# Two layers of a conv-FFN backbone on one core: raw operands kept and products chained in PSUM around the down-projection

## The chip, the cores and the metric

The kernel runs as one program on one NeuronCore of a Trainium2 chip. The metric is the device time of one execution in microseconds. The five engines work side by side, each in the order in which its own instructions were recorded: TensorE (PE), VectorE (DVE), ScalarE (ACT), GpSimd (POOL) and SyncE (SP, which here only issues DMAs). They wait for one another by semaphores. DMAs are issued from SP, from ACT and from POOL; those from POOL go to queue q0, which can add what it moves to what lies at the destination ("accumulate" below), the others to q1.

## The reference

Two layers. Each has a token-mixing sub-layer (attention, a gated linear recurrence, a Fourier mix) and then the gated ConvFFN that the change touches:

```python
def conv_ffn(h, w_up, conv_w, conv_b, w_down):
    u = h @ w_up                                   # 1024 -> 2 x 2816
    up = jnp.pad(u, ((0, 0), (1, 1), (0, 0)))
    u = up[:, :-2] * conv_w[0] + up[:, 1:-1] * conv_w[1] + up[:, 2:] * conv_w[2] + conv_b
    a, g = jnp.split(u, 2, axis=-1)
    return (a * jax.nn.silu(g)) @ w_down           # 2816 -> 1024

    x1 = layer_norm(ALPHA * x + g1 * mix, ln1_g[l], ln1_b[l])
    ffn = conv_ffn(x1 * (1 + sc2) + sh2, w_up[l], conv_w[l], conv_b[l], w_down[l])
    x = layer_norm(ALPHA * x1 + g2 * ffn, ln2_g[l], ln2_b[l])
```

There are 1024 latent tokens and 256 context tokens, all in float32. The change is in the ConvFFN of the latent tokens.

## The kernel before

**Arithmetic.** A float32 product is made of three passes of a reduced type. Every operand is split into a rounded part, hi (a cast on ACT), and the rest, lo (a subtraction), and `mm3` (L156 to L160) issues lo·hi, hi·lo and hi·hi. One such product of a 128x128 and a 128x512 tile is three matmuls.

**Two stages with seven products.** Both matrix products of the FFN are done as a 2x2 block product with seven block products in place of eight: A11..A22 are quarters of one operand, B11..B22 of the other, S1..S4 and T1..T4 are sums of quarters. The up-projection comes first, for 22 column pairs j, then the down-projection.

**Up-projection** (`up_weights`, `up_all`). For each j the weights are the A side. `operand` (L1204) makes S1 to S4 on DVE, `splits` casts hi on ACT (L1216) and subtracts lo on POOL (L1217). The B side, the tokens, lies in SBUF already split. Each product is 12 matmuls into one PSUM bank "p" of 128x512 (`up_product`). ORDER (L1186) has the products as A11, A12, S1, S2, S3, A22, S4. `up_all` then forms the outputs by seven DVE sums (L1232) of a bank and a part of the SBUF tiles U[0] and U[1] (each 128x1026: an early half of 512 tokens, a late half, and borders), after ACT has copied A11's bank to U[0]'s late half (L1265). `gate(j)` reads U: a width-3 convolution (`conv`: one ACT operation L1102, then two DVE operations L1105, for each of four half tiles), SiLU on ACT, and a DVE product (L1244 or L1246), whose result is stored to DRAM as `act`. For j below EARLY=6 the products A11 and A12 were made earlier (`up_early`), stored in DRAM ("parked") and are loaded to U[0]'s late half (L1259, L1271), one after the other. PE gets the operands up to five products ahead.

**Down-projection** (`down_operands`, `down_all`). The operands are now `act` (A side) and w_down (B side), each quarter 11 chunks of 128 rows, 2.88 MB. Seven phases run one after the other, in the order of DOWN (L1287): P1 = A11·B11, P7 = S3·T3, P6 = S2·T2, P4 = A22·T4, P5 = S1·T1, P3 = S4·B22, P2 = A12·B21. Each has six steps (one chunk, then five times two), of 12 matmuls for each chunk, into four PSUM banks; so a phase is 132 matmuls. A raw operand is loaded to a rotating buffer ("raw" for weights, "araw" for activations, three of these). Operands that are sums are held in SBUF: X (weights) and Y (activations), six tiles each. In P1 `hold` (L1322, L1326) loads X with B22 and Y with A11 and adds B12 and A21 by accumulate DMAs from POOL (L1319). Each later sum comes from the one before by one more accumulate DMA (`next_sum`), issued after the step's split has read the tile. S1 and T1, in P5, are a load into araw and into raw and an accumulate onto each. Splits are a cast on ACT (L1347) and a subtraction on DVE (L1348). At the end of a phase `combine` reads the four banks: a copy on ACT in P1 (L1403), sums on DVE (L1371) later. PLAN (L1428) has `load_r` load the residual rows r of the later four token tiles in steps 2 to 5 of P1 and multiply and add on DVE (L997, L998).

The order on each engine is the order of the recorded program, in which a recording layer hoists splits and sums ahead of the matmuls that use them; no engine passes an instruction that waits.

Of the kernel before, what the change touches and what calls it, by code (L numbers as in the profile page):

```python
# [11 lines left out]
F32 = mybir.dt.float32  # L12
# [84 lines left out]
def hybrid_backbone_kernel(ctx: ExitStack, tc: tile.TileContext, A: dict, out: bass.AP):  # L97
# [1072 lines left out]
    def up_product(w, b, bank):  # L1170
        acc = psu([P, HALF], "pu", bank)
        for k in range(4):
            mm3(acc, tuple(t[:, k, :] for t in w), tuple(t[:, k, :] for t in b), k == 0, k == 3)
# [12 lines left out]
    ORDER = (("A11", "B11"), ("A12", "B21"), ("S1", "T1"), ("S2", "T2"), ("S3", "T3"), ("A22", "T4"), ("S4", "B22"))  # L1186

    def up_weights(l, fp):
# [19 lines left out]
        def splits(todo):  # L1208
            for n, (j, nm) in enumerate(todo):
# [7 lines left out]
                nc.gpsimd.tensor_tensor(out=lo, in0=src, in1=f32(hi), op=ALU.subtract)  # L1217
# [5 lines left out]
    def up_all(l, fp, todo, ws, h, parked, act, bg):  # L1223
# [25 lines left out]
        for j, a, b in todo:  # L1249
            if a == [o for o in ORDER if j >= EARLY or o[0][0:2] != "A1"][0][0]:  # L1250
                p1, u2, u3, u4 = U[0][:, late], U[1][:, early], U[1][:, late], U[0][:, early]

                sums = (("u2", u2, "S2", "p1", ALU.add, ()), ("C11", p1, "A12", "p1", ALU.add, ("u2",)),
                        ("u3", u3, "S3", "u2", ALU.add, ()), ("u4", u4, "S1", "u2", ALU.add, ()),
                        ("C22", u2, "S1", "u3", ALU.add, ("u4",)), ("C21", u3, "u3", "A22", ALU.subtract, ("C22",)),
                        ("C12", u4, "S4", "u4", ALU.add, ()))
                got = {"p1": p1}
# [8 lines left out]
            for o, dst, x, y, op, after in sums:
                if o not in got and all(n in got for n in (x, y) + after):
                    add(dst, got[x], got[y], op)
                    got[o] = dst
                    if o == "u2" and j < EARLY:  # L1270
# [20 lines left out]
    def down_operands(l, f1, f2, f3, act):  # L1291
        X, Y = {}, {}
# [13 lines left out]
        def load_w(fw, q, ks):  # L1306
            count[0] += 1
            t = (fw if count[0] % 2 else wp).tile([P, 1024], F32, tag="raw", bufs=2, name="raw")[:, 0:512 * len(ks)]
            nc.sync.dma_start(out=halves(t), in_=w_part(q, ks))
            return t  # L1310

        def load_a(q, ks, eng=None, first=False):
            t = (wp if first else f1[0]).tile([P, 1024], F32, tag="raw" if first else "araw", bufs=2 if first else 3,
                                              name="araw")[:, 0:512 * len(ks)]
            (eng or nc.sync).dma_start(out=halves(t), in_=a_part(q, ks))
            return t
# [5 lines left out]
        def hold(n, ks):  # L1322

            for held, pl, nm, part, x, y in ((X, f3[0], "X", w_part, "B22", "B12"), (Y, f2[0], "Y", a_part, "A11", "A21")):
                held[n] = pl.tile([P, 512 * len(ks)], F32, tag=f"{nm}{n}", bufs=1, name=nm)
                nc.sync.dma_start(out=halves(held[n]), in_=part(x, ks))  # L1326
                plus(held[n], part(y, ks))

        def side_a(q, n, ks, first):
            if q[0] == "A":  # L1330
                return load_a(q, ks, nc.scalar if q == "A11" and n < 2 and not first else None, first)
            return plus(load_a("A22", ks), a_part("A21", ks)) if q == "S1" else Y[n]

        def side_b(fw, q, n, ks):
            if q[0] == "B":
                return load_w(fw, q, ks)
            return plus(load_w(fw, "B11", ks), w_part("B12", ks)) if q == "T1" else X[n]

        def next_sum(q, n, ks):
            if q in ("S3", "S2"):  # L1340
                plus(Y[n], a_part("A22" if q == "S3" else "A12", ks))
            if q in ("T3", "T2"):
                plus(X[n], w_part("B11" if q == "T3" else "B21", ks))
# [7 lines left out]
        def split_w(fw, q, n, ks):  # L1351
# [13 lines left out]
    def down_all(l, fp, fa, ops, ready, y1, rows, finish, deferred, halfway):  # L1365
# [65 lines left out]
        for x, (p, qa, qb) in enumerate(DOWN):  # L1431
# [385 lines left out]
```

## Time and profile before

| | |
|---|---|
| median of 3 runs | 3408.84 us (3407.7 to 3414.72) |
| profiled execution | 3419.26 us, span 3417.4 us |
| PE busy | 3116.8 us (91%) |
| DVE busy | 2417.0 us (71%) |
| ACT busy | 1550.2 us (45%) |
| POOL busy | 1261.6 us (37%) |
| POOL, lo of the up-projection (L1217) | 176 from S of 1618 ns mean, 108 from raw of 1392 ns |
| queue q1 | 409.24 MB |
| queue q0 (accumulates among it) | 55.80 MB |
| up-projection, layer 0 and layer 1 | about 895 to 1405 us, about 2680 to 3133 us |
| down-projection, layer 0 and layer 1 | about 1405 to 1680 us, about 3133 to 3417 us |

Read the engines' totals as averages over stages with different limits. The stage rows come from the trace: a stretch of time with the busy time of each engine in it, the groups by line, the waits (who waited for whom, how long, how often, the longest), the chain that ended last, and the timeline of one engine.

### The profile page before, as it was taken

The page shows a single profiled execution, that of the slowest core. Times are in us where ns is not written, and L with a number is a line of the kernel's source. Part 1 is how long each engine was busy: PE and PEld are TensorE (multiplying, and loading weights), DVE is VectorE, ACT ScalarE, POOL GpSimd, SP SyncE. Part 2 cuts the span into 40 slices and gives each one's busy share as a digit, 9 for nine tenths or more (in the row PEclk, how much of TensorE's full clock was granted, in tenths as well). Part 3 has the DMA queues.
Part 4 walks back from the last instruction along what each step waited for, and adds up shares of the span by engine and source line. Part 5 has one row for each costly group of instructions (what it writes and reads, how often), then busy time and mean ns, then how long its engine had stood idle before and what let it go on. Part 6 is the DMA issues. An engine that isn't in the chain of part 4 may idle for free.

```text
span 3417.4 us, 55716 instructions
## 1 busy us (share of the span) xinstructions
PE 3116.8 (91%) x20897; PEld 2540.3 (74%) x20897; DVE 2417.0 (71%) x4171; ACT 1550.2 (45%) x3105; POOL 1261.6 (37%) x1134
## 2 busy tenths in 40 slices
PE   6999998989889999798899999998978889998896
PEld 4879976778766777576798888876766668776675
DVE  4614568887698888547876755668877798886568
ACT  4325556664443433233465435655642434443332
POOL 3522105422464444241235341115435545553323
PEclk9999999999989999899999999998998899999898
DMA  7643122117764443698775432122035642225993
GB/s 214 204 153 85 49 93 58 40 44 220 224 183 142 129 129 122 192 246 205 242 209 178 131 105 70 47 90 65 21 112 159 195 130 74 79 81 159 255 227 123
DMA packets 457412, 468.60 MB, mean 137 GB/s; under 512 B 32244, under 2 KB 343989, under 8 KB 457143
## 3 DMA queue, kind: packets, MB, share of 16 engines
q1 hardware_dynamic: 422294, 409.24, 37.9%
q0 software_dynamic: 34848, 55.80, 8.6%
q8 instruction: 165, 2.70, 0.3%
q14 instruction: 105, 0.85, 0.1%
HBM read 370.41 MB, written 94.54 MB: 136 GB/s over the span
## 4 chain that ended last, share of the span: by engine, by line
PE 28%; DVE 16%; DMA 14%; issue 9%; POOL 9%; ACT 3%; SPq 0%; POOLq 0%; DVEq 0%; ACTq 0%
PE pu L158 4%; POOL wlo L1217 4%; PE pu L159 4%; PE pu L160 4%; DMA araw<-act 3%; DMA X<-in_w_down_dram 3%; DVE cv L1105 3%; DMA raw<-in_w_down_dram 2%; PE ps_t L602 2%; PE ps_s L566 1%; DVE wlo L1348 1%; PE ps_o L612 1%; DVE U L1232 1%; DMA hraw<-yT 1%; DVE S L1204 1%
## 5 line engine op out<-in xcount | busy, mean ns | idle before, releaser
L1217 POOL TENSOR_TENSOR wlo<-S,whi 128x512 fp32r<-128x512 f32 x176 | 283.0, 1618 | 281.9 <-ACT whi L1216 268.2
L1105 DVE SCALAR_TENSOR_TENSOR cv<-U,cw,cv 128x512 f32<-128x512 f32 x352 | 326.0, 974 | 33.9 <-ACT cv L1102 33.8
L158 PE MATMUL pd<-whi,wlo 128*128 128x512 f32 x616 | 248.5, 411 | 58.5 <-DVE wlo L1348 50.2
L569 DVE TENSOR_REDUCE mx<-ps_s 128x1 f32<-128x512 f32 (+1 forms) x400 | 222.2, 588 | 108.0 <-PE ps_s L567 106.9
L608 DVE TENSOR_TENSOR pl<-ps_t,ph 128x512 fp32r<-128x512 f32 x328 | 223.0, 686 | 86.2 <-ACT ph L607 84.1
L145 POOL TENSOR_TENSOR wlo<-raw,whi 128x1024 fp32r<-128x1024 f32 x69 | 168.1, 2438 | 298.6 <-ACT whi L144 298.5
L602 PE MATMUL ps_t<-ident,p 128*128 128x128 f32 x1312 | 263.1, 284 | 13.6 <-DVE pl L608 8.1
L159 PE MATMUL pd<-wlo,whi 128*128 128x512 f32 x616 | 250.9, 407 | 17.5 <-DVE wlo L1348 14.3
L576 ACT ACTIVATE p<-ps_s,mx 128x512 f32<-128x512 f32 (+1 forms) x400 | 243.2, 617 | 52.0 <-DVE mx L572 42.3
L607 ACT CAST ph<-ps_t 128x512 fp32r<-128x512 f32 x328 | 190.9, 589 | 162.3 <-PE ps_o L614 80.4
L1102 ACT ACTIVATE cv<-U,cb,cw 128x512 f32<-128x512 f32 x176 | 137.6, 815 | 258.1 <-DVE U L1232 210.5
L160 PE MATMUL pd<-whi 128*128 128x512 f32 x616 | 249.2, 405 | 0.0
L158 PE MATMUL pxs<-whi,hlo 128*128 128x256 f32 x752 | 221.5, 295 | 5.8 <-DVE hraw L1524 4.3
L159 PE MATMUL pxs<-wlo,hhi 128*128 128x256 f32 x752 | 216.5, 288 | 0.5 <-DVE wlo L145 0.4
L160 PE MATMUL pxs<-whi,hhi 128*128 128x256 f32 x752 | 216.4, 288 | 0.0
L612 PE MATMUL ps_o<-pl,V 128*128 128x256 f32 x656 | 201.1, 323 | 6.7 <-DVE pl L608 4.8
L1217 POOL TENSOR_TENSOR wlo<-raw,whi 128x512 fp32r<-128x512 f32 x108 | 149.7, 1392 | 129.8 <-ACT whi L1216 115.6
L602 PEld LDWEIGHTS ps_t<-ident,p 128*128 128x128 f32 x1312 | 165.1, 143 | 36.8 <-DVE pl L608 10.9
L158 PEld LDWEIGHTS pd<-whi,wlo 128*128 128x128 f32 x616 | 119.3, 195 | 94.1 <-DVE wlo L1348 56.2
L1232 DVE TENSOR_TENSOR U<-pu,U 128x512 f32<-128x512 f32 x252 | 167.4, 686 | 26.9 <-PE pu L160 18.5
L614 PE MATMUL ps_o<-ph,V 128*128 128x256 f32 x656 | 183.2, 297 | 0.0
L556 POOL DMA_DIRECT2D qt<-QT x72 | 40.5, 563 | 374.6 <-PE ps_s L567 277.1
(395 smaller groups left out, 9423.6 us busy)
## 6 DMA issues: line engine op xcount, KB each, us to landing
raw<-in_w_up_dram SPq DMA_DIRECT2D x144, 512.0 KB
raw<-in_w_ada_dram SPq DMA_DIRECT2D x96, 512.0 KB
raw<-in_w_down_dram SPq DMA_DIRECT2D x62, 512.0 KB
act<-cv SPq DMA_DIRECT2D x88, 256.0 KB
araw<-act SPq DMA_DIRECT2D x40, 512.0 KB
raw<-in_w_in_dram SPq DMA_DIRECT2D x36, 512.0 KB
X<-in_w_down_dram POOLq DMA_DIRECT2D x30, 512.0 KB, 17.2
Y<-act POOLq DMA_DIRECT2D x30, 512.0 KB, 17.8
```

What stands on the lines that cost most here:

```text
L158: nc.tensor.matmul(o, lhsT=al, rhs=bh, start=start, stop=False)
L159: nc.tensor.matmul(o, lhsT=ah, rhs=bl, start=False, stop=False)
L160: nc.tensor.matmul(o, lhsT=ah, rhs=bh, start=False, stop=stop)
L569: nc.vector.tensor_reduce(out=mx[:, j:j + 1], in_=t[:, 0:n], axis=AX.X, op=ALU.max)
L576: nc.scalar.activation(out=t, in_=sc[j][:, 0:n], func=AF.Exp, bias=mx[:, 3:4], accum_out=su[:, h, j:j + 1])
L602: nc.tensor.transpose(t[:, ss, h, :], in_=ps2[h][2 * s2 + ss], identity=ident)
L607: nc.scalar.copy(ph, tv)
L608: nc.vector.tensor_tensor(out=pl, in0=tv, in1=f32(ph), op=ALU.subtract)
L612: nc.tensor.matmul(o, lhsT=V[:, s, kv, 1:3, :].rearrange("p a c -> p (a c)"), rhs=pl[:, ss, :], start=(s == 0), stop=False)
L1105: nc.vector.scalar_tensor_tensor(out=o, in0=u[:, tap:tap + n], scalar=convw[l][tap][:, c:c + 1], in1=o, op0=ALU.mult, op1=ALU.add)
L1217: nc.gpsimd.tensor_tensor(out=lo, in0=src, in1=f32(hi), op=ALU.subtract)
L1232: nc.vector.tensor_tensor(out=o, in0=x, in1=y, op=op)
```

## The change

In the **up-projection** lo of the weights is subtracted on DVE instead of POOL, in `up_early` too for every j. ORDER has S2 ahead of S1. `up_product` takes `onto`: the product is then accumulated in the PSUM bank of an earlier product, so S2 goes onto A11's bank, S3 onto S2's, S4 onto S1's. For j from 6 on, ACT copies three banks to U (A11, S2 and S3; L1264 and L1272 of the changed kernel) and DVE makes four sums (L1234) instead of seven; for j below 6 DVE makes five instead of six.

In the **down-projection** Y is loaded with A11 and nothing is added to it in P1; P1 itself reads Y from its third step on (A11 is loaded twice for the first two). A21 is then loaded to araw and added to Y by DVE for P7 (L1349 of the changed kernel). A22 is loaded during P7 to a new set of tiles Z (four in raw buffers, two in araw), added to Y by DVE for P6, used as it is in P4, and gets A21 by an accumulate DMA to be S1 in P5. T1 is made in X: X is loaded anew with B11 after P4's split and B12 accumulated. A12 is accumulated onto Y for S4 after P6. So each layer has 36 accumulate DMAs instead of 48 and 12 DVE sums more. `load_r` of the later four tiles moves from P1's steps 2 to 5 to P6's.

```diff
@@ mm3: skip_group_check=onto on each of the three matmuls
+    def up_product(w, b, bank, onto=None):
+        acc = psu([P, HALF], "pu", bank) if onto is None else onto
         for k in range(4):
+            mm3(acc, ..., k == 0 and onto is None, k == 3, onto is not None)
-        w = w_split(w_up_cols(l, 0, j), (KD, P), eng=nc.vector if j < 3 else None)
+        w = w_split(w_up_cols(l, 0, j), (KD, P), eng=nc.vector)
-    ORDER = (("A11", "B11"), ("A12", "B21"), ("S1", "T1"), ("S2", "T2"), ("S3", "T3"), ("A22", "T4"), ("S4", "B22"))
+    ORDER = (("A11", "B11"), ("A12", "B21"), ("S2", "T2"), ("S1", "T1"), ("S3", "T3"), ("A22", "T4"), ("S4", "B22"))
-                nc.gpsimd.tensor_tensor(out=lo, in0=src, in1=f32(hi), op=ALU.subtract)
+                nc.vector.tensor_tensor(out=lo, in0=src, in1=f32(hi), op=ALU.subtract)
...
+            onto = {"S2": "A11", "S3": "S2", "S4": "S1"}.get(a)
+            t = got[a] = up_product(ahead.pop(0), h[b], "p", got.get(onto))
             if a == "A11":
                 nc.scalar.copy(p1, t)
+            elif a == "A12":
+                add(p1, p1, t)
+            elif a in ("S2", "S3"):
+                o = u2 if a == "S2" else u3
+                if j < EARLY:
+                    add(o, t, p1)
+                else:
+                    nc.scalar.copy(o, t)
+                if a == "S3":
+                    if j < EARLY:
                         nc.sync.dma_start(out=p1, in_=parked[j, 1])
+                    add(U[1][:, early], got["S1"], u3)
+            elif a == "A22":
+                add(u3, u3, t, ALU.subtract)
+            elif a == "S4":
+                add(u2, t, u2)
...
-                plus(held[n], part(y, ks))
+        def hold_a(n, ks):
+            Y[n] = f2[0].tile([P, 512 * len(ks)], F32, tag=f"Y{n}", bufs=1, name="Y")
+            load(Y[n], a_part("A11", ks))
+        def side_a(p, q, n, ks, first):
+            if p == "P1":
+                return Y[n] if n in Y else load(raw_a(ks, first), a_part(q, ks), nc.scalar if n < 2 and not first else None)
+            if p in ("P7", "P6"):
+                x = Z[n] if p == "P6" else load(raw_a(ks), a_part("A21", ks))
+                nc.vector.tensor_tensor(out=Y[n], in0=Y[n], in1=x, op=ALU.add)
+            return load(raw_a(ks), a_part(q, ks)) if p == "P2" else Z[n] if p in ("P4", "P5") else Y[n]
+        def next_a(fw, p, n, ks):
+            if p == "P7":
+                Z[n] = load(raw_w(fw, ks) if n < 4 else raw_a(ks), a_part("A22", ks))
+            elif p == "P4":
+                plus(Z[n], a_part("A21", ks))
+            elif p == "P5":
+                plus(Y[n], a_part("A12", ks))
+        def next_b(p, n, ks):
+            if p in ("P7", "P6"):
+                plus(X[n], w_part("B11" if p == "P7" else "B21", ks))
+            elif p == "P4":
+                plus(load(X[n], w_part("B11", ks)), w_part("B12", ks))
...
-        PLAN = [(("P1", m + 2), load_r, (NCT + 4 + m,)) for m in range(4)] + [
+        PLAN = [(("P6", m + 2), load_r, (NCT + 4 + m,)) for m in range(4)] + [
```

The order on two places of DVE, both in layer 1. First the seam between one j and the next in the up-projection, j from 6 on. In the kernel before, U_29145 is U[0] and U_29146 is U[1]; the last convolutions of one j (L1105), its products (L1246, L1244), the sums S for a later j (L1204), and then the first sum of the next j:

```order
L1105 SCALAR_TENSOR_TENSOR cv_31893<-U_29145,cw_337,cv_31893 128x512
L1105 SCALAR_TENSOR_TENSOR cv_31904<-U_29145,cw_329,cv_31904 128x512
L1246 TENSOR_TENSOR cv_31893<-cv_31893,cv_31888 128x512
L1105 SCALAR_TENSOR_TENSOR cv_31904<-U_29145,cw_337,cv_31904 128x512
L1204 TENSOR_TENSOR S_32152<-raw 128x512
L1244 SCALAR_TENSOR_TENSOR cv_31904<-cv_31904,cv_31899 128x512
L1204 TENSOR_TENSOR S_32156<-S_32152,raw 128x512
L1204 TENSOR_TENSOR S_32158<-raw 128x512
L1232 TENSOR_TENSOR U_29146<-pu,U_29145 128x512
L1232 TENSOR_TENSOR U_29145<-pu,U_29145 128x512
```

In the changed kernel U_29049 is U[0] and U_29050 is U[1]; the last sum of a j (S4's bank, onto U[0]) and the convolutions that read U[0], L1106 being the convolution, then what follows:

```order
L1234 TENSOR_TENSOR U_29049<-pu,U_29049 128x512
L1106 SCALAR_TENSOR_TENSOR cv_31422<-U_29050,cw_337,cv_31422 128x512
L1106 SCALAR_TENSOR_TENSOR cv_31427<-U_29049,cw_329,cv_31427 128x512
L1106 SCALAR_TENSOR_TENSOR cv_31433<-U_29050,cw_337,cv_31433 128x512
L1106 SCALAR_TENSOR_TENSOR cv_31427<-U_29049,cw_337,cv_31427 128x512
L1106 SCALAR_TENSOR_TENSOR cv_31438<-U_29049,cw_329,cv_31438 128x512
L1248 TENSOR_TENSOR cv_31427<-cv_31427,cv_31422 128x512
L1106 SCALAR_TENSOR_TENSOR cv_31438<-U_29049,cw_337,cv_31438 128x512
L1219 TENSOR_TENSOR wlo<-S_31534,whi 128x512
L1246 SCALAR_TENSOR_TENSOR cv_31438<-cv_31438,cv_31433 128x512
```

Before, what stands behind the convolutions on DVE is the sum of S2's bank with U[0] (U_29146<-pu,U_29145). In the changed kernel that sum is gone: after the last convolution that reads U[0], ACT copies A11's bank to U[0]'s late half, and S2's matmuls, which add to that bank, come after the copy. On PE, S2's 12 matmuls stand 29 or 30 matmuls behind the last one of the j before (12 of A11, 12 of A12, 5 or 6 of S1).

Then DVE from the last steps of P1 into P7. In the kernel before (L1348 is lo, r the residual rows):

```order
L1348 TENSOR_TENSOR wlo<-araw,whi 128x1024
L997 TENSOR_TENSOR r<-r,ga 128x1024
L998 TENSOR_TENSOR r<-r,ba 128x1024
L1348 TENSOR_TENSOR wlo<-araw,whi 128x1024
L1348 TENSOR_TENSOR wlo<-raw,whi 128x1024 x2
L1348 TENSOR_TENSOR wlo<-X,whi 128x512
L1348 TENSOR_TENSOR wlo<-X,whi 128x1024
L997 TENSOR_TENSOR r<-r,ga 128x1024
L998 TENSOR_TENSOR r<-r,ba 128x1024
L1348 TENSOR_TENSOR wlo<-araw,whi 128x1024
L1348 TENSOR_TENSOR wlo<-Y,whi 128x512
L1348 TENSOR_TENSOR wlo<-Y,whi 128x1024
```

In the changed kernel (L1349 is the new sum, L1373 is lo):

```order
L1349 TENSOR_TENSOR Y<-Y,araw 128x512
L1373 TENSOR_TENSOR wlo<-Y,whi 128x1024
L1373 TENSOR_TENSOR wlo<-X,whi 128x512
L1349 TENSOR_TENSOR Y<-Y,araw 128x1024
L1373 TENSOR_TENSOR wlo<-Y,whi 128x512
L1349 TENSOR_TENSOR Y<-Y,araw 128x1024
L1373 TENSOR_TENSOR wlo<-X,whi 128x1024
L1349 TENSOR_TENSOR Y<-Y,raw 128x512
L1349 TENSOR_TENSOR Y<-Y,araw 128x1024
L1373 TENSOR_TENSOR wlo<-Y,whi 128x1024
L1373 TENSOR_TENSOR wlo<-X,whi 128x1024
L1349 TENSOR_TENSOR Y<-Y,araw 128x1024
```

The residual rows have left the place. In it stand the sums of Y with A21 (araw) and with A22 (raw), the first of them ahead of the last lo of P1 (wlo<-Y, 128x1024, the second row), and the sums for later steps stand ahead of the lo of earlier ones.

## Rows read from the trace of the kernel before

**Rows 1.** Windows: us, busy PE, PEld, DVE, ACT, POOL; clock; DMA share; GB/s.
```profile
2957.30:2997.80 40.50, 38.76 (x170) 31.47 (x169) 35.11 (x42) 17.14 (x29) 21.07 (x15) 1.00 0.25 78
1120.00:1165.00 45.00, 45.00 (x216) 33.53 (x217) 37.56 (x46) 17.37 (x28) 20.36 (x14) 1.00 0.45 140
3140.00:3170.00 30.00, 15.79 (x57) 11.98 (x56) 7.17 (x6) 6.60 (x8) 4.13 (x5) 0.73 1.02 295
3230.00:3260.00 30.00, 30.00 (x133) 24.71 (x132) 11.93 (x12) 10.32 (x12) 13.40 (x12) 1.00 1.12 215
```

**Rows 2.** Chain of waits, 2880 to 2960 us: start, us, engine and line.
```profile
2892.95 2.54 POOL wlo L1217 x2
...
2933.44 2.55 POOL wlo L1217 x2
```

**Rows 3.** Groups by line and form, 2876.4 to 2957.3 us (four j).
```profile
L1105 DVE SCALAR_TENSOR_TENSOR cv<-U,cw,cv 128x512 f32<-128x512 f32 x32 | 29.5, 968 | 3.8 <-ACT cv L1102 3.8
L1217 POOL TENSOR_TENSOR wlo<-S,whi 128x512 fp32r<-128x512 f32 x16 | 27.0, 1692 | 28.8 <-ACT whi L1216 28.8
L1232 DVE TENSOR_TENSOR U<-pu,U 128x512 f32<-128x512 f32 x24 | 16.0, 686 | 0.3
```

**Rows 4.** Timeline, layer 1, j below 6: gate's product on DVE; lo on POOL.
```profile
2734.24 0.68 DVE L1244 SCALAR_TENSOR_TENSOR cv<-cv,cv 128x512 f32<-128x512 f32 x1
...
2820.98 4.70 POOL L1217 TENSOR_TENSOR wlo<-S,whi 128x512 fp32r<-128x512 f32 x3 [8.26 <-ACT whi L1216]
...
2824.45 1.78 DVE L1244 SCALAR_TENSOR_TENSOR cv<-cv,cv 128x512 f32<-128x512 f32 x1
```

**Rows 5.** Timeline of SP and of DVE: a parked product loaded and used.
```profile
2791.63 0.34 SPq L1259 DMA_DIRECT2D U<-up  x1
...
2795.72 0.69 DVE L1232 TENSOR_TENSOR U<-pu,U 128x512 f32<-128x512 f32 x1 [1.46 <-DMA U<-up]
```

**Rows 6.** Timeline of PE, up-projection of layer 1: a pause (in brackets).
```profile
2913.01 0.47 PE L158 MATMUL pu<-B21h,wlo 128*128 128x512 f32 x1 [1.80 <-DVE U L1232]
...
2915.08 0.63 PE L159 MATMUL pu<-B21l,whi 128*128 128x512 f32 x1
```

**Rows 7.** Timeline of PE, down-projection of layer 1: another pause.
```profile
3293.52 0.50 PE L158 MATMUL pd<-whi,wlo 128*128 128x512 f32 x1 [1.90 <-DVE wlo L1348]
3293.86 0.39 PE L159 MATMUL pd<-wlo,whi 128*128 128x512 f32 x1
```

**Rows 8.** Queues of the whole span: packets, MB, share of 16 engines.
```profile
q1 hardware_dynamic: 422294, 409.24, 37.9%
q0 software_dynamic: 34848, 55.80, 8.6%
```

**Rows 9.** Chain of waits, down-projection of layer 1.
```profile
3175.08 13.54 DMA araw<-act
```

**Rows 10.** Waits, 3119 to 3330 us: us in total, times, longest.
```profile
DVE r L997 <- DMA r<-y: 33.8, 4, 19.6
...
PE pd L158 <- DVE wlo L1348: 23.5, 4, 13.1
```

**Rows 11.** Ends of phases in layer 1, ACT and DVE: P1, P7, P5.
```profile
3196.20 1.95 ACT L1403 COPY p<-pd 128x512 f32<-128x512 f32 x3 [4.00 <-PE pd L160]
...
3226.42 2.80 DVE L1371 TENSOR_TENSOR v<-pd,p 128x512 f32<-128x512 f32 x4
...
3322.68 0.69 DVE L1371 TENSOR_TENSOR v<-v,pd 128x512 f32<-128x512 f32 x1
```

**Rows 12.** The same of layer 0.
```profile
1469.04 1.99 ACT L1403 COPY p<-pd 128x512 f32<-128x512 f32 x3 [2.60 <-PE pd L160]
...
1499.84 2.79 DVE L1371 TENSOR_TENSOR v<-pd,p 128x512 f32<-128x512 f32 x4
...
1610.10 0.68 DVE L1371 TENSOR_TENSOR v<-v,pd 128x512 f32<-128x512 f32 x1
```

**Rows 13.** Line L1348 in layer 1's down-projection: ns min, median, max.
```profile
L1348 DVE TENSOR_TENSOR wlo<-Y,whi x18: 683/1225/2044, 3190.9 to 3351.7; 128x1024 fp32r<-128x1024 f32 x15, 128x512 fp32r<-128x512 f32 x3
```

More of the change, by code (lines that the diff above doesn't have):

```diff
@@ L1168, in combined_halves @@
             yield
[L1170 to L1171 removed]
+    def up_product(w, b, bank, onto=None):
+        acc = psu([P, HALF], "pu", bank) if onto is None else onto
         for k in range(4):
[L1173 removed]
+            mm3(acc, tuple(t[:, k, :] for t in w), tuple(t[:, k, :] for t in b), k == 0 and onto is None, k == 3,
+                onto is not None)
         return acc
     def up_early(l, j, h, rp, tag, parked):
[L1178 removed]
+        w = w_split(w_up_cols(l, 0, j), (KD, P), eng=nc.vector)
         p1, c11 = (rp.tile([P, HALF], F32, tag=tag, bufs=2, name="early") for _ in range(2))
@@ L1250, in up_all @@
             if a == [o for o in ORDER if j >= EARLY or o[0][0:2] != "A1"][0][0]:
[L1251 to L1257, printed above, removed]
+                got = {}
                 if j < EARLY:
-                    nc.sync.dma_start(out=p1, in_=parked[j, 0])
+                    nc.sync.dma_start(out=U[0][:, late], in_=parked[j, 0])
             while len(ahead) < 5:
                 ahead.append(next(ws, None))
-            t = up_product(ahead.pop(0), h[b], "p")
-            got[a] = t
+            onto = {"S2": "A11", "S3": "S2", "S4": "S1"}.get(a)
+            t = got[a] = up_product(ahead.pop(0), h[b], "p", got.get(onto))
+            p1, u2, u3 = U[0][:, late], U[0][:, early], U[1][:, late]
             if a == "A11":
                 nc.scalar.copy(p1, t)
[L1266 to L1270, printed above, removed]
-                        nc.sync.dma_start(out=p1, in_=parked[j, 1])
+            elif a == "A12":
[8 more added lines that the diff above has]
+                    if j < EARLY:
+                        nc.sync.dma_start(out=p1, in_=parked[j, 1])
+                    add(U[1][:, early], got["S1"], u3)
[3 more added lines that the diff above has]
+                add(u2, t, u2)
             for _ in range(1 if a in ("A22", "S3") or j % 2 and a == "S2" else 0):
@@ L1291, in down_operands @@
     def down_operands(l, f1, f2, f3, act):
-        X, Y = {}, {}
+        X, Y, Z = {}, {}, {}
         count = [0, 0]
@@ L1304, in halves, with raw_w, load, raw_a @@
             return t.rearrange("p (k c) -> p k c", c=512)
-        def load_w(fw, q, ks):
[L1307 to L1316, printed above, removed]
+        def raw_w(fw, ks):
+            count[0] += 1
+            return (fw if count[0] % 2 else wp).tile([P, 1024], F32, tag="raw", bufs=2, name="raw")[:, 0:512 * len(ks)]
+        def load(t, part, eng=None):
+            (eng or nc.sync).dma_start(out=halves(t), in_=part)
+            return t
+        def load_w(fw, q, ks):
+            return load(raw_w(fw, ks), w_part(q, ks))
+        def raw_a(ks, first=False):
+            return (wp if first else f1[0]).tile([P, 1024], F32, tag="raw" if first else "araw", bufs=2 if first else 3,
+                                                 name="araw")[:, 0:512 * len(ks)]
         def plus(t, part):
@@ L1320, in plus @@
             return t
[L1322 to L1326, printed above, removed]
-                plus(held[n], part(y, ks))
[L1329 to L1332, printed above, removed]
@@ new lines, in hold_b @@
+        def hold_b(n, ks):
+            X[n] = f3[0].tile([P, 512 * len(ks)], F32, tag=f"X{n}", bufs=1, name="X")
+            plus(load(X[n], w_part("B22", ks)), w_part("B12", ks))
+        def side_a(p, q, n, ks, first):
[5 more added lines that the diff above has]
+            return load(raw_a(ks), a_part(q, ks)) if p == "P2" else Z[n] if p in ("P4", "P5") else Y[n]
@@ L1696, in hybrid_backbone_kernel @@
             ops = down_operands(l, f1, f2, f3, act_d)
-            ready = [ops[0](DOWN[0][1], n, STEPS[n], True) for n in range(IN_WP)]
+            ready = [ops[0](*DOWN[0][0:2], n, STEPS[n], True) for n in range(IN_WP)]
             h2s.close()
```

44 lines of the change are left out of this document (20 added, 24 removed).

## Prediction

> **What bounds the kernel now.** I read the page first: PE is busy for 91% of the span, so a gain has to come from the stretches where PE is not busy or not at full clock. Then the windows, stage by stage. In the up-projection of layer 1, j from 6 on, PE works 38.76 of 40.50 us at clock 1.00 with DVE at 35.11; in layer 0 the same stage has PE full, 45.00 of 45.00 us. At the start of the down-projection PE works 15.79 of 30.00 us, the clock is at 0.73 and the DMA share 1.02: the transfers set the pace. In P6 PE is full again, 30.00 us with 133 matmuls at clock 1.00 [rows 1]. That row gives one matmul, 30.00/133 = 0.2256 us; so a j of 84 matmuls cannot take less than 18.95 us, and a phase of 132 not less than 29.8 us.
>
> The chain of waits says what sets the j of layer 1: POOL's lo, with two pairs 40.49 us apart for two j, 20.25 us each, 1.30 above PE's floor [rows 2]. The groups by line show the other side of it: 1.69 us for POOL's 128x512 lo, and 0.97 us for DVE's convolution [rows 3]. One and the same DVE product takes 0.68 us with POOL idle and 1.78 us while POOL runs three lo [rows 4]. In the down-projection the chain goes through loads of activations, the last of P1 landing at 3175.08 + 13.54 = 3188.6 us [rows 9], and the ends of the phases give the lengths: P1 is read out at 3196.20, P7 at 3226.42, P5 at 3322.68 [rows 11].
>
> **The up-projection, j from 6 on, layer 1 (16 j).** POOL's seven lo per j go. DVE then has 4 sums S, 7 lo, 8 convolutions, 2 products and 4 sums of U, 25 instructions against 21. At the 0.68 us that such an instruction takes with POOL idle [rows 4] that is 17.0 us; before it was 35.11/2 = 17.6 us per j, since POOL made DVE's instructions longer. DVE stays below PE's 18.95, but not by much. ACT has two more copies of 1.95/3 = 0.65 us [rows 11] on 17.14/2 = 8.6 per j [rows 1]; it is hidden.
>
> What the change adds is a wait. S2 goes onto A11's bank, so its matmuls wait for ACT's copy of the bank, and the copy writes where the last convolutions of the j before still read. In the order of the changed kernel the way from that j's last product to the copy is one sum, six convolutions and one product on DVE, 8 x 0.68 = 5.4 us, and the copy, 0.65: 6.1 us with nothing for the hand-overs. PE has 29.5 matmuls to do meanwhile, 6.65 us. It fits by half a microsecond. If the convolutions stay at 0.97 us [rows 3], it is 6 x 0.97 + 2 x 0.69 + 0.65 = 7.85, and PE waits 1.2 us in each j. The ends are 18.95 us per j (-21 us over 16 j) and 18.95 + 1.2 = 20.15 plus what the clock takes after each such pause (the second rival). Behind the waiting T2 matmuls stands the rest of S1 and all that follows, so a wait there is lost in full. I take 19.45, half a microsecond above the floor, because the DVE row without POOL is the nearer one: -0.8 x 16 = **-13 us**.
>
> **Layer 0, j from 6 on.** PE has no gap to give [rows 1]; it also does the modulation's products there. The gain is nothing; a tenth of a microsecond of the new wait per j makes **+2**, with 0 and 1.2 x 16 = +19 as the ends.
>
> **j below 6.** Before, a j takes (2824.45 - 2734.24)/5 = 18.04 us in layer 1 [rows 4]. Here the way round is a parked product's load after the last convolution that reads U[0], 2795.72 - 2791.63 = 4.1 us [rows 5], S2's sum 0.69, and now also S3's twelve matmuls behind that sum, since they go onto its bank (2.71), then A22 (2.71), S4 (2.71), a sum 0.69 and seven DVE instructions, 4.8: 18.4 us and the hand-overs, about 19. That is +1 for five j in layer 1 and less in layer 0: **+3**, between -5 (DVE's shorter instructions) and +10. Lo in `up_early` on DVE I cost at nothing: it lies beside PE's and DMA's work of the preparation, and without that cover it is at most the six splits that move, 6 x 1.2 = 7 us [rows 13].
>
> **P1.** The queues' rows price a megabyte: q1 0.379 x 3417.4/409.24 = 3.16 us, q0 0.086 x 3417.4/55.80 = 5.27 us of all engines together, 1.66 times as much [rows 8]. A quarter is 2.88 MB: 9.1 us plain, 15.2 us accumulated. Before, P1 moves B11, A11, B22 and A11 again, and accumulates B12 and A21: 4 x 9.1 + 2 x 15.2 = 66.8 us, and 2 MB of r, 6.3. After it moves B11, A11, B22, three chunks of A11 again (2.5 us) and accumulates B12: 27.3 + 2.5 + 15.2 = 45.0. That is 28 us less work for the queues in the stage that they bound. DVE's 33.8 us of waiting for r go from P1 too [rows 10]. PE itself needs 29.8 us from about 3137, so P1 cannot end before 3167; I take 3172 for 3196, -24 us.
>
> **P7 gives most of that back.** P7 now needs A21 as a load of its own and a DVE sum before its split: 5 x 1.22 + 0.68 = 6.8 us by the lo of the same shape [rows 13], which DVE can bear. But the loads come late: A21 (9.1 us) and the first four tiles of Z (about 5.8) stand behind P1's 45, and the accumulation of B11 onto X runs beside them. 3123 + 45 + 9 + 6 = 3183, and with part of the 15.2 us of X, about 3190. In DVE's order the lo of P7's third step stands behind the sum with A21's last tile, and that tile's load waits for a free araw buffer. So PE has two steps (36 matmuls, 8 us, to 3180) and then waits to about 3193; the remaining 96 matmuls and a smaller pause end P7 at about 3219, against 3226: **-7 us** for P1 and P7 together. The ends: -28 (nothing given back) and +8 (each of the last steps waits for its own load, 6 x 2.5 us more).
>
> **P6, P4 and P5.** Before, 3322.68 - 3226.42 = 96.3 us [rows 11] for 3 x 29.8 = 89.4. P6 loses its accumulation of A22 and of A21; P4 and P5 lose what P5 waited for in rotating buffers; against that the r loads and DVE's waits for them now lie in P6, where DVE is less loaded (11.93 of 30.00 us [rows 1]) but where a lo behind such a wait makes PE wait, as in P1, where PE waits 23.5 us for lo in 4 places [rows 10]. I take 93: **-3**; ends -7 (no pause left) and +20 (the longest wait for r, 19.6 us [rows 10], hits PE whole).
>
> **Layer 0** has the same phases, P7 taking 1499.84 - 1469.04 = 30.8 and P6 to P5 1610.10 - 1499.84 = 110.3 us [rows 12], 21 above PE's floor, so there is more to get from fewer accumulations: -4 up to P7 and -8 for the rest, **-12**, between -35 and +15. P3 and P2 keep their operands and I cost them at nothing; Y's accumulation of A12 comes one phase earlier than it is needed.
>
> **Sum.** -13 + 2 + 3 - 7 - 3 - 12 = -30. The profiled execution took 3419.26 us, 1.9 more than its span, which makes 3389; it lies 10.4 above the median of the runs. On the median's footing: 3408.8 - 30 = 3379, and I say **3378 us**.
>
> **Rivals.** First, *the down-projection keeps it*: A21 comes early enough, and P1's 24 us are not given back. For it: after the change the queues have 28 us less to move before P7. Against it: the order of DVE, in which the last A21 sum stands ahead of P7's third lo. Layer 0 does the same: -13 + 5 - 24 - 3 - 24 = -59, 3350.
>
> Second, the other side, *the PSUM chain makes PE pause in every j*: S2's matmuls reach the head of PE's queue before the copy. A pause costs itself and the clock. In the trace a pause of 1.80 us in the up-projection is followed by matmuls of 0.63 us, the lower of the two clock levels [rows 6]; the row is one of eight such in a row, 0.24 us longer each than 0.39, 1.9 us lost. But a pause of 1.90 us in the down-projection is followed by one of 0.39 at the full clock [rows 7], so a fall is not certain. With a pause of 2 us and the fall, a j takes 18.95 + 2 + 1.9 = 22.85, +2.6 x 16 = +42 in layer 1 and less, perhaps +10, in layer 0, whose PE has the modulation's products to put in between: 42 + 10 - 22 = +30, **3439**. It decides from about 1 us of pause per j on, that is when DVE's eight instructions behind the last product take 6.5 us instead of 5.4. The Trainium skill has a rule beside it ("TensorE: Matmul & The Clock Gate", section "A second HAM failure mode: psum-queue depth-cycling"): short idles of PE between groups of matmuls that cycle through banks make the clock go up and down, and the loss is in the throughput and not in the single matmul. Rows 6 agrees with it and rows 7 does not; by the rule alone every j would pay.
>
> Third, *no net change*: P7's and P6's new waits take back all that P1 gives, in both layers, and the up-projection's -8 is eaten by j below 6 and layer 0: about 3408.
>
> **How the numbers follow.** My forecast has a chance of 0.54, its own range is 3360 to 3400 (half of each term's ends, in root sum). The first rival has 0.20, the second 0.16, the third 0.10. A change within 0.2%, 6.8 us, can't be told from none. All of the first two of these cases is faster (0.74), the third rival is the same (0.10), the second slower (0.16). The range from 3336 to 3415 takes in the forecast, the first rival and the third, and leaves out most of the second.
>
> **What would show it.** In the up-projection of layer 1 the chain of waits goes through PE, not POOL; lo is 0.6 to 0.7 us on DVE; the convolutions drop from 0.97 to about 0.75; and T2's first matmul waits at most 0.5 us in each j. If that wait is over 1 us and matmuls of 0.63 follow, the second rival holds. In the down-projection P1 is read out 20 to 28 us earlier after its start; PE's longest pause of P7 stands ahead of its third step and ends with DVE's lo; DVE's wait for r is in P6. If P7 has no pause over 5 us, the first rival holds. If P5's end comes no earlier than before, the third.

## Result and the profile after

The changed kernel takes 3348.22 us (median of 4 runs, 3341.59 to 3357.33) against 3411.09 (4 runs, 3407.7 to 3414.72): a ratio of 0.9819, 95% interval 0.9805 to 0.9833, 62 us less. The forecast was 3378, range 3336 to 3415: the direction is right, but the gain is twice the 30 us of the sum, as much as in the first rival (3350). The time lies outside the 3360 to 3400 that the forecast gave itself; the whole range holds it because it was drawn to take in that rival. The profiled span is 3345.0 us, 72.4 less; 7.5 of these lie in a stretch that the change doesn't touch (from the end of layer 0's P2 to layer 1's first early product on PE, 981.7 us before, 974.2 after; it took 974 to 985 in the kernels below), so single profiles aren't read closer than that.

The page of the changed kernel, busy time, two queues, and the convolution's group (line, operation, shapes, count, busy us, mean ns, idle before):

```profile
PE 3087.2 (92%) x20897; PEld 2517.1 (75%) x20897; DVE 2379.1 (71%) x4377; ACT 1581.3 (47%) x3169; POOL 780.8 (23%) x820
...
q1 hardware_dynamic: 420118, 405.05, 38.6%
q0 software_dynamic: 28832, 44.27, 7.1%
...
L1106 DVE SCALAR_TENSOR_TENSOR cv<-U,cw,cv 128x512 f32<-128x512 f32 x352 | 246.7, 746 | 12.8 <-ACT cv L1103 12.7
```

DVE has 206 instructions more and 38 us less busy time: the convolution's mean fell from 974 ns to 746. The Trainium skill says why ("SBUF — State Buffer", section "Who interferes with whom"): a DVE instruction with two inputs in SBUF contends with a GpSimd instruction that reads SBUF, one with at most one such input, outside the modes that take two ports, doesn't. The traces agree: the sum of a PSUM bank and U took 686 ns before [rows 3] and 690 after.

Windows of the changed kernel (columns as in [rows 1]): two j of layer 1, one stretch of layer 0, and layer 1's P1:

```profile
2931.40:2970.20 38.80, 38.80 (x169) 31.23 (x168) 31.90 (x51) 19.64 (x32) 0.00 (x0) 1.00 0.26 82
1155.00:1200.00 45.00, 45.00 (x214) 33.78 (x213) 34.38 (x56) 20.01 (x33) 0.00 (x0) 1.00 0.42 128
3083.00:3122.70 39.70, 34.14 (x133) 27.01 (x134) 18.82 (x22) 15.57 (x20) 7.83 (x7) 0.87 1.07 310
```

The first answers to the first of [rows 1]: PE no longer pauses, two j take 38.8 us instead of 40.5, DVE works 31.9 us instead of 35.1. In the third PE still waits in P1, but works 34 of 40 us, where it worked 16 of 30 before.

Where the time went is best counted by PE alone. Line L158 (L159 after) issues 44 matmuls per phase, so every 44th start is the start of a phase; DVE's reading of a phase's banks, by which [rows 11, 12] cut it, lags by what DVE waits for. In us:

| | P1 | P7 | P6 | P4 | P5 | P3 | P2 |
|---|---|---|---|---|---|---|---|
| layer 0 before | 62.2 | 30.8 | 30.8 | 31.3 | 43.5 | 34.4 | 35.8 |
| layer 0 after | 44.3 | 35.4 | 30.8 | 30.8 | 30.8 | 32.6 | 33.6 |
| layer 1 before | 65.7 | 30.3 | 30.1 | 30.3 | 35.8 | 36.7 | 34.8 |
| layer 1 after | 39.6 | 38.3 | 30.1 | 30.3 | 30.1 | 36.7 | 34.8 |

(P2 is counted to the last of these starts.) P1 and P7 together get shorter by 13.3 and 18.1 us, P5 by 12.7 and 5.7, P3 and P2 of layer 0 by 4.0. The up-projection by `gate`'s first product of a j on DVE, from j = 0 to 5, from 5 to 20, and the mean period from 11 to 19 (us):

| | layer 0: j 0-5 | j 5-20 | period | layer 1: j 0-5 | j 5-20 | period |
|---|---|---|---|---|---|---|
| before | 95.5 | 324.8 | 21.78 | 90.2 | 295.8 | 20.23 |
| after | 99.6 | 310.7 | 21.47 | 99.7 | 282.2 | 19.30 |
| no chain (below) | 82.7 | 318.5 | 21.44 | 75.7 | 282.9 | 19.30 |

The period of layer 1 before is that of [rows 2]. From the first `gate` product to the down-projection's first matmul the change gains 10.0 us in layer 0 and 0.2 in layer 1.

Single columns of this table have to be read with care, because `gate` on DVE doesn't follow PE at a fixed distance. From j = 5 to 11 of layer 0, before and after:

```profile
1066.57:1198.15 131.58, 128.86 (x608) 95.77 (x607) 110.93 (x142) 51.76 (x84) 62.18 (x42) 0.99 0.41 126
1070.15:1187.79 117.64, 117.64 (x548) 86.63 (x547) 95.44 (x157) 57.72 (x95) 0.00 (x0) 1.00 0.43 131
```

PE is busy nearly throughout in both, but does 60 matmuls fewer after: 60 x 0.21 = 12.6 of the 14 us are work that fell ahead of `gate`'s j = 5. What layer 0 did win are PE's waits from `gate`'s first product on, for the modulation's operands before,

```profile
PE pada L246 <- DMA raw<-in_w_ada_dram: 6.7, 3, 5.1
PE padat L264 <- DVE adar L256: 4.6, 1, 4.6
PE padat L264 <- DVE mod L265: 3.1, 3, 2.0
```

and for the products' own sums and lo after:

```profile
PE pu L159 <- DVE U L1234: 3.4, 3, 1.9
PE pu L159 <- DVE wlo L1219: 2.0, 1, 2.0
```

P1 and P7 of layer 1 by their queues (packets, MB, share of 16 engines), first before, 3132 to 3228 us:

```profile
q0 software_dynamic: 5159, 9.88, 56.1%
q1 hardware_dynamic: 7735, 17.02, 50.4%
```

then after, 3083 to 3161 us:

```profile
q1 hardware_dynamic: 7447, 15.46, 54.7%
q0 software_dynamic: 3603, 6.89, 50.4%
```

In both the queues are full all along (DMA share 1.07 and 1.05). A megabyte of q0 costs 0.561 x 96/9.88 = 5.5 us of them before and 0.504 x 78/6.89 = 5.7 after, one of q1 2.8 and 2.8: twice as much, where the whole span gave 1.66. The 3.0 MB of q0 and 1.6 MB of q1 that went are 17 + 4 = 21 us, and 18.1 were won.

### The profile page after: what moved, and what is told of

Same layout as the page of the kernel before. It is cut to its first block, busy times and chain, and to the rows that moved or that the text cites. A ratio compares the mean times of both kernels' runs of the same rounds, so it can differ in the third digit from the quotient of the medians.

```text
span 3345.0 us, 55178 instructions
## 1 busy us (share of the span) xinstructions
PE 3087.2 (92%) x20897; PEld 2517.1 (75%) x20897; DVE 2379.1 (71%) x4377; ACT 1581.3 (47%) x3169; POOL 780.8 (23%) x820
## 4 chain that ended last, share of the span: by engine, by line
PE 46%; DVE 12%; DMA 5%; POOL 3%; issue 2%; ACT 2%; SPq 0%; POOLq 0%; DVEq 0%; ACTq 0%
PE pu L159 8%; PE pu L160 8%; PE pu L161 8%; PE pd L159 3%; PE pd L160 3%; PE pd L161 3%; PE ps_t L603 2%; DMA araw<-act 2%; DVE cv L1106 1%; PE ps_s L567 1%; PE ps_o L613 1%; PE ps_s L568 1%; PE ps_o L615 1%; PE pws L159 1%; DVE wlo L1373 1%
## 5 line engine op out<-in xcount | busy, mean ns | idle before, releaser
L1331 POOL DMA_DIRECT2D X<-in_w_down_dram x48 | 57.0, 1188 | 1022.5 <-DMA X<-in_w_down_dram 944.7
L159 PE MATMUL pd<-whi,wlo 128*128 128x512 f32 x616 | 243.6, 402 | 17.5 <-DVE wlo L1373 10.4
L1106 DVE SCALAR_TENSOR_TENSOR cv<-U,cw,cv 128x512 f32<-128x512 f32 x352 | 246.7, 746 | 12.8 <-ACT cv L1103 12.7
L159 PE MATMUL pxs<-whi,hlo 128*128 128x256 f32 x752 | 220.9, 294 | 5.7 <-DVE hraw L1552 4.3
L145 POOL TENSOR_TENSOR wlo<-raw,whi 128x1024 fp32r<-128x1024 f32 x63 | 153.5, 2439 | 281.1 <-ACT whi L144 281.0
L1218 ACT CAST whi<-S 128x512 fp32r<-128x512 f32 x176 | 106.1, 618 | 146.4 <-PE pu L161 110.4
L144 ACT CAST whi<-raw 128x1024 fp32r<-128x1024 f32 x130 | 135.8, 1047 | 81.9 <-DMA raw<-in_w_up_dram 30.1
L567 PE MATMUL ps_s<-KT,qt 128*128 128x512 f32 (+1 forms) x400 | 149.8, 405 | 6.5 <-ACT p L577 3.1
L159 PEld LDWEIGHTS pd<-whi,wlo 128*128 128x128 f32 x616 | 117.6, 192 | 49.7 <-DVE wlo L1373 13.1
```

The lines of the kernel that those rows point to most:

```text
L567: nc.tensor.matmul(t[:, 0:n], lhsT=qt[:, h % (2 * QT_PAIRS), :], rhs=KT[:, 2 * kv + 1, s0:s0 + n], start=True, stop=False)
L1106: nc.vector.scalar_tensor_tensor(out=o, in0=u[:, tap:tap + n], scalar=convw[l][tap][:, c:c + 1], in1=o, op0=ALU.mult, op1=ALU.add)
```

## The experiments

Each ratio is to the kernel before on the same chip, and microseconds against the changed kernel are differences of these ratios (the changed kernel has 0.9819).

**One part alone.** The down-projection alone (the up-projection as before):

> The up-projection of the kernel before with the down-projection of the changed one. My theory after the result: most of the gain is the down-projection's. In the traces layer 0's gains 38 us from its first matmul to layer 1 and layer 1's 23, the up-projections 10.5 and 1; so this kernel stands about 52 us under the kernel before (3359, ratio 0.985). The rival is the forecast's split, up-projection -8 and down-projection -22 with the rest coming from how the two meet: about -25 (3386, ratio 0.993).

3366.1 us, ratio 0.9872 (0.9849 to 0.9895): -44. And the up-projection alone:

> The up-projection of the changed kernel with the down-projection of the kernel before. Theory: about -10 us (3400, ratio 0.997), layer 0's. Rival (the two parts need each other, since DVE's and POOL's work of the one frees the other): no gain, or a loss of up to 10 us.

3406.3 us, ratio 0.9985 (0.9969 to 1.0002): -5, and not told from nothing. So the down-projection brings the gain, as my theory had it, a little less than its 52; its P5, 30.8 and 30.1 us, is that of the changed kernel. The up-projection's parts nearly cancel. Apart they make 49 of the 62 us; the rest is within the two intervals taken together.

**The residual rows back in P1** (one word of PLAN):

```diff
-        PLAN = [(("P6", m + 2), load_r, (NCT + 4 + m,)) for m in range(4)] + [
+        PLAN = [(("P1", m + 2), load_r, (NCT + 4 + m,)) for m in range(4)] + [
```

> The changed kernel with the residual rows loaded in P1 again, steps 2 to 5, in place of P6. Theory: P1 is bound by its transfers, 2 MB of r are 6.3 us of the queues and stand ahead of operands, so P1 ends 6 to 10 us later in each layer, and P7 absorbs some of it: +8 to +16 us in all (ratio 1.0025 to 1.005 to the changed kernel). Rival, the move is worth nothing because P7 waits for its loads anyway: within 3 us of the changed kernel.

3373.7 us, ratio 0.9903 (0.9874 to 0.9931): +29 by the ratios, more than I had expected. In its trace P1 and P7 take 8.7 us more in layer 0 and 9.8 in layer 1; the rest of the 29 I can't place, since the profiled execution is the shortest of the four, with a span only 15.4 us over the changed kernel's. I had counted 2 MB of r. But the rows that r needs go with it, in layer 1 ga, ba, go, bo and g of 0.5 MB each, in layer 0 ga, ba and g. In layer 1 ga's load is issued at 3096.38 us here, in P1, and at 3129.25 in the changed kernel, in P7. DVE's wait for r, over P1 and P7 of layer 1, is there again:

```profile
DVE r L998 <- DMA r<-y: 12.3, 3, 8.8
```

In the changed kernel it is 5.0 us in two waits, in P6, and costs nothing there: P6 is 30.1 and 30.8 us, PE's bare need.

**A21 accumulated in P1 again**, in place of a load and a sum on DVE:

```diff
-                nc.vector.tensor_tensor(out=Y[n], in0=Y[n], in1=x, op=ALU.add)     # x: A21 from araw, in P7
+            if p == "P1" and n >= 2:
+                plus(Y[n], a_part("A21", ks))                                     # in hold_a for n < 2
```

> The changed kernel with A21 added to Y by accumulate DMAs in P1, as before, in place of a load and a DVE sum in P7; A22, S1, T1 and the residual rows stay as in the changed kernel. Theory (P1 and P7 are set by the queues, and an accumulated byte costs 1.66 plain ones): P1 and P7 together, 79.7 and 77.9 us by PE's first matmuls, become 4 to 8 us longer in each layer, +8 to +16 in all. Rival (DVE's sums ahead of lo set P7, and A21's load by three buffers): P7 goes back to 31 us, P1 grows by less, and the kernel is up to 8 us faster.

3381.8 us, ratio 0.9907 (0.9888 to 0.9925): +30. P1 and P7 take 98.5 and 93.8 us, 19 and 16 more; the theory's sign, twice its size. Most of it, 17.8 and 13.4 us, is in P7, whose second step (12 matmuls into it) waits. PE in layer 1 (start, us, ..., in brackets its pause and the releaser):

```profile
3167.88 0.80 PE L159 MATMUL pd<-whi,wlo 128*128 128x512 f32 x1 [19.24 <-DVE wlo L1376]
```

In the changed kernel the pause at this place is

```profile
3130.01 0.80 PE L159 MATMUL pd<-whi,wlo 128*128 128x512 f32 x1 [4.44 <-DVE wlo L1373]
```

The three araw buffers and DVE's sums ahead of lo, on which I had put P7's wait, are worth at most those 4.4 us. But what the 19 us wait for is not A21 either. SP and ACT ahead of that lo:

```profile
3140.06 0.55 SPq L977 DMA_DIRECT2D ga<-in_ln_g_dram  x1
...
3164.57 1.06 ACT L979 ACTIVATE ga<-ga 128x1024 f32<-128x1024 f32 x1 [23.72 <-DMA ga<-in_ln_g_dram]
3165.54 1.03 ACT L1375 CAST whi<-Y 128x1024 fp32r<-128x1024 f32 x1
```

ga is a row of the layer norm. In this program ACT scales it ahead of the casts of P7's second step, in the changed kernel behind them, and ACT waits for its load, 24.7 us in layer 0. The last of the six accumulations onto Y was issued at 3143.02 us and none took over 14.1 to land, so Y was ready by 3157.1. What A21 adds is work for the queues: ga's load took 24.5 us here, with X's and Y's accumulations beside it, and 8.9 in the changed kernel. By the stage's prices 2.9 MB accumulated in place of loaded are 2.9 x (5.7 - 2.8) = 8 us per layer; with ga elsewhere in ACT's order it was not tried. Nor can this cost be added to that of r as a share of the gain: the two make 27.5 and 25.7 us of P1 and P7, where the change won 13.3 and 18.1.

**S1 in rotating buffers again** (A22 loaded anew in P5, A21 accumulated on it there):

```diff
+            if p == "P5":
+                return plus(load(raw_a(ks), a_part("A22", ks)), a_part("A21", ks))
-            elif p == "P4":
-                plus(Z[n], a_part("A21", ks))
```

> The changed kernel with S1 made as before: A22 loaded again to araw in P5 and A21 accumulated there, in place of the accumulation onto Z during P4. By the times of PE's first matmul in each phase, P5 took 43.5 and 35.8 us before and 30.8 and 30.1 after. Theory: what kept P5 waiting were sums in rotating buffers, whose load, accumulation and split follow one another with three buffers only; here P5 takes 36 to 42 us again and the kernel is 8 to 20 us slower than the changed one. Rival (T1's raw buffers or the r loads were it): P5 stays at 31 and the time within 3 us.

3365.1 us, ratio 0.9859 (0.9837 to 0.9881): +14. P5 takes 34.9 and 36.7 us, P3 in layer 0 38.1 for 32.6. In P5 of layer 1, ACT waits for araw:

```profile
ACT whi L1372 <- DMA araw<-act: 25.5, 5, 12.6
```

So S1 in its rotating buffers accounts for all of P5's wait before in layer 1 (5.7 us, here 6.6), in layer 0 for 4.1 of 12.7 with 5.5 more in P3; T1's half was not tried.

**The early products' lo back on POOL** (`eng=nc.vector if j < 3 else None`) and **lo of the first five products on POOL**:

> The changed kernel with the early products' lo on POOL again for j of 3 and more. In the changed kernel PE stands still for 18.9 and 20.0 us at the start of the up-projection, waiting for the hi of S2, whose sum waits on DVE. Theory: DVE is full there because of the lo that moved to it; with POOL doing it the two pauses shrink to about 8 us each and the kernel gains some 15 to 20 us (3330). Rival: the pause comes from S2 standing first in the order and from the lo of the weights, which all go through DVE; then it stays above 15 us and the time within 4 us of the changed kernel.

3352.0 us, ratio 0.9832 (0.981 to 0.9855): no gain, the rival held; PE's first pauses stay at 18.3 and 18.7 us.

> The changed kernel with lo of the first five products of each up-projection on POOL, the others on DVE. It follows from the run with the early products' lo on POOL, which did not shorten the two pauses of 19 and 20 us: in DVE's order the lo of the first S2 stands behind all the preparation of the tokens. Theory: with those five lo on POOL, PE starts S2 while the last quarter of T2 is still being made, the two pauses fall to about 10 us each, and the kernel gains 12 to 20 us (ratio to the changed kernel 0.994 to 0.996). Rival: PE waits for T2 itself (its last quarter comes at the end of the preparation), and nothing is gained: within 4 us.

3357.3 us, ratio 0.9841 (0.9815 to 0.9866): no gain either, though PE does start earlier. PE in layer 1, the first S2 and the first S3:

```profile
2657.86 0.79 PE L159 MATMUL pu<-T2h,wlo 128*128 128x512 f32 x1 [5.77 <-ACT T2h L1148]
...
2674.59 0.77 PE L159 MATMUL pu<-T3h,wlo 128*128 128x512 f32 x1 [4.85 <-DVE U L1234]
```

It waits for T2's later quarters, as the rival said, and then for the sum of S2. The pause of 20 us, the longest in the changed kernel's trace, costs nothing: what it waits for is the preparation, which ends no sooner.

**lo on POOL, products chained:**

```diff
-                nc.vector.tensor_tensor(out=lo, in0=src, in1=f32(hi), op=ALU.subtract)
+                nc.gpsimd.tensor_tensor(out=lo, in0=src, in1=f32(hi), op=ALU.subtract)
```

> The changed kernel with all lo of the up-projection on POOL, as before, and the products still chained. Theory (the up-projection's gain is POOL's removal; POOL makes DVE's convolutions longer): the convolutions go back from 0.75 to 0.97 us, S2 then waits 1 us or more for A11's copy in each j, and layer 1's j from 6 on takes 20.3 us or more, in place of 19.4; with layer 0 +20 to +40 us on the changed kernel. Rival (the gain is the chain's fewer DVE sums): the j stays below 19.8 and the time within 8 us of the changed kernel.

3513.0 us, ratio 1.0292 (1.0273 to 1.0311): +161, four times the most that I had expected. The period is 24.5 us in layer 1 and 24.0 in layer 0. Four j of layer 1, 3040 to 3138 us, by groups:

```profile
L1106 DVE SCALAR_TENSOR_TENSOR cv<-U,cw,cv 128x512 f32<-128x512 f32 x32 | 31.5, 1030 | 4.4 <-ACT cv L1103 4.4
...
L159 PE MATMUL pu<-T2h,wlo 128*128 128x512 f32 x16 | 9.6, 602 | 12.8 <-ACT U L1264 12.8
```

This is the second rival whole: the convolutions at 1.03 us, 3.2 us of pause ahead of S2 in each j, and then slow matmuls. Their mean of 602 ns, against 409 in layer 1 of the changed kernel from 2850 to 3070 us, is the lower clock: the granted clock is 0.58 from 3039.9 to 3044.0 us, at S2, near the lower level of 1.2 GHz, and 1.00 from 3050 to 3060. The Trainium skill's rule on short idles agrees ("TensorE: Matmul & The Clock Gate", section "A second HAM failure mode: psum-queue depth-cycling").

**No chain: own banks and seven sums, lo on DVE** (`up_all`'s sums and `up_product` as before):

> The changed kernel with each product in a bank of its own and the seven DVE sums of before, lo on DVE and the order of the products as in the changed kernel. Theory: DVE gets 28 instructions of 0.68 us or 19.0 us per j, as much as PE's floor, without POOL; the j from 6 on takes 19.4 to 20.0 us; +2 to +15 us on the changed kernel. Rival: the chain costs what it saves (S2's wait), and this kernel is up to 10 us faster than the changed one, most of it in the j below 6.

3316.7 us, ratio 0.972 (0.9697 to 0.9742), clear of the changed kernel's interval: the chain costs 0.0099 of 3411, 34 us, and this kernel beats both. Against the theory DVE's 28 instructions don't hold PE up: in two j it works 37.86 of 39.11 us and PE 39.11:

```profile
2879.05:2918.16 39.11, 39.11 (x172) 32.07 (x172) 37.86 (x62) 18.75 (x30) 0.00 (x0) 1.00 0.31 94
```

By the table above the gain lies up to j = 5, 16.9 and 24.0 us (the 7.8 that layer 0 loses after it are moved work again). From `gate`'s first product to the down-projection PE is not busy for 6.4 and 15.5 us in the changed kernel, and for 0.7 in both layers here. In the changed kernel, one j of layer 1 on SP, DVE and PE:

```profile
2745.38 0.39 SPq L1255 DMA_DIRECT2D U<-up  x1
...
2750.69 0.69 DVE L1234 TENSOR_TENSOR U<-pu,U 128x512 f32<-128x512 f32 x1 [2.81 <-DMA U<-up]
...
2751.44 0.50 PE L159 MATMUL pu<-T3h,wlo 128*128 128x512 f32 x1 [3.64 <-DVE U L1234]
...
2753.01 0.63 PE L161 MATMUL pu<-T3h,whi 128*128 128x512 f32 x1
```

The parked product is loaded after `gate`, S2's sum waits for it, S3's matmuls wait for the sum because they go onto its bank, and after the pause they run at 0.63 us. Without the chain PE has no pause named from `gate`'s first product on.

**The parked product earlier**, chain kept (from POOL, to U[1]'s late half):

```diff
-                    nc.sync.dma_start(out=U[0][:, late], in_=parked[j, 0])
+                    nc.gpsimd.dma_start(out=U[1][:, late], in_=parked[j, 0])
-                    add(o, t, p1)
+                    add(o, t, u3)
```

> The changed kernel, chain and all, but for j below 6 the parked A11 product is loaded to U[1]'s late half, whose last reader comes four DVE instructions earlier, and from POOL, which has nothing else there, so that it isn't queued behind the store of gate's last product on SP. The sums of S2 and S3 read it there. Theory (the parked load stands on the way from one j to the next): the five j fall from 99.6 and 99.7 to 80 to 90 us, and the kernel gains 15 to 30 us. Rival (S2's sum waits for gate's last reader of its own place, U[0]'s early half, as late as for the load): less than 6 us.

3331.0 us, ratio 0.9759 (0.9739 to 0.9779): -20. The five j take 88.8 and 86.9 us, so that load is on the path. POOL still waits for the convolutions, once in each j:

```profile
2737.10 0.54 POOL L1255 DMA_DIRECT2D U<-up  x1 [16.29 <-issue]
2754.22 0.54 POOL L1255 DMA_DIRECT2D U<-up  x1 [16.59 <-DVE cv L1106]
```

**Chain only for j from 6 on** (`onto` None below):

> The changed kernel with products chained only for j from 6 on; for j below 6 each has a bank of its own and the sums of before. Without any chain the kernel took 3316.7 us against 3348.2. From the first product of gate to that of j=5, five j took 82.8 and 75.7 us there (layer 0, layer 1), 99.6 and 99.7 in the changed kernel. Theory: all of the chain's cost lies in j below 6, where S3's matmuls wait for S2's sum and that for the parked product; so this kernel takes 3310 to 3325 us, as without a chain, and the five j 76 to 84 us. Rival: the chain costs in all j by S2's wait for A11's copy; then about half is won, 3330 to 3340.

3332.2 us, ratio 0.976 (0.974 to 0.9779): the rival's time, but not its cause, since no T2 matmul waits; and my theory fell in part. The five j are as short as without a chain, 82.5 and 74.7 us, but j 5 to 20 of layer 1 take 293.0 for 282.9; the period from 11 to 19 is 19.41, hardly longer. The loss starts with a pause of 4.22 us at j = 6, which DVE's lo ends:

```profile
2760.77 0.80 PE L159 MATMUL pu<-T4h,wlo 128*128 128x512 f32 x1 [4.22 <-DVE wlo L1219]
```

The changed kernel has the same pause at the same product, the first T4 of a chained j:

```profile
2768.43 0.50 PE L159 MATMUL pu<-T4h,wlo 128*128 128x512 f32 x1 [3.15 <-DVE wlo L1219]
```

So part of the chain's cost lies where it begins, and not in the j below 6. Whether the chain itself moves DVE's order there, or the hoisting of another program, stays open.

**No chain and early loads:**

> The kernel without a chain (own banks, lo on DVE), with the parked products loaded early from POOL, A11's to U[1]'s late half and A12's to U[0]'s. Theory: without a chain PE isn't held by the parked load, five j take 82.8 and 75.7 us, of which PE's 60 matmuls each are 67.7; so 5 us per layer or less are left to gain: 3306 to 3317 us. Rival: no gain, 3317, since the sums' places in U are free no earlier.

3316.7 us, ratio 0.9724 (0.9699 to 0.9749): the rival, nothing gained. Without the chain PE doesn't wait for the load.

## Why the prediction was right or wrong

- **Right: direction, and that P1 ends by its transfers.** From its first matmul P1 of layer 1 is 26 us shorter (forecast 24 at its end).
- **Wrong: "P7 gives most of that back".** This step failed by its size. I had 7 us left of P1 and P7 in layer 1 and 4 in layer 0, measured are 18.1 and 13.3. I laid Z's loads, A21's and X's accumulation one behind the other and put P7's third step 61 us after P1's first matmul; it comes 3138.9 - 3083.1 = 56 us after it. The pause is ended by lo, as I had it, but stands a step earlier (second step, at 3130.0 us, 12 matmuls into P7), and its length is 4.4 us, with 1.0 at the third, and not 13. The range held the time by its width, not by this term.
- **Wrong: the price of an accumulation.** I took it from the whole span (1.66 plain ones). In the stage that it binds it is 2.0, which makes A21's accumulation 8 us per layer. The 16 and 19 measured hold a wait for ga as well.
- **Mis-sized: "P6, P4 and P5".** -3 and -8 became -5.7 and -13.2, all but half a microsecond of it in P5. I read the lengths from DVE's sums; by PE, P6 never waited, and r in P6 is free. P3 and P2, which I had at nothing, gave 4.0 us in layer 0 and none in layer 1.
- **The up-projection** was -8 by the sum and is -10 by the tables, but not by my terms. The steady j of layer 1 came as forecast, 19.30 us for 19.45. PE is full there, 38.80 us for 169 matmuls or 0.2296 each, so this is its floor: the 0.2256 that I took from P6 made mine, 18.95, too low. Over j from 5 to 20 it is 13.6 us (forecast 13), about half of it moved work (29 matmuls). Layer 0's 14.1 from j = 5 to 20, where I had +2, are nearly all work that moved to the j before; PE had 2.7 us to give from j = 5 to 11, so "PE full" was nearly right. The j below 6 lost 4.1 and 9.5 where I had 3 in all, with 59 and 28 matmuls more in them. What layer 0 won are the waits for the modulation's operands, which I had no term for.
- **The rivals.** The first gives the time, by its condition only in part: P7 has no pause over 5 us, but P1's gain was not kept whole (4.6 and 8.0 go back). The second, the PSUM chain, I had placed at S2 in every j. In the changed kernel T2's matmuls never wait over 0.5 us in the steady j; it acts at S3 in the j below 6, where I wrote the very path down and priced it at 3 against the kernel before, and at the first chained j. Against the same kernel without a chain it costs 34 us. And its condition was named rightly: at convolutions of 1.03 us it decides everywhere.

## What to carry to other kernels

Price a DMA kind in the stage that it binds, and ask what else waits for a load in the same queues: a row of the layer norm, ahead of a cast in ACT's order, held PE for 19 us. Cut phases by the engine that is the bound; cut by another one, work moves from one phase to the next and looks like a gain. Accumulating onto a bank that another engine still has to read makes that reader, and all that it waits for, a wait of PE; before chaining for fewer sums, see whether the sums cost anything: here a j takes 19.30 us with seven and with four.

## What was not expected of the hardware

A DMA that accumulates took 5.5 to 5.7 us of the queues per MB, a plain one 2.8, in the same stretch. DVE's 128x512 operation with two SBUF inputs averaged 746 ns with POOL idle and 974 to 1030 with POOL's subtractions beside it. PE's pause of 20 us was free, and one of 3.6 us was not.
